# Down-projection of sixteen of 22 blocks by Strassen's scheme in two of three token groups

## The chip, the core and the metric

One core of a Trainium2 chip runs the whole program. The core has a matrix engine (TensorE, PE in the profile) that multiplies into PSUM banks, a vector engine (VectorE, DVE), a scalar engine (ScalarE, ACT), a helper (GpSimd, POOL), and a queue of transfers that is issued by SyncE (SP); a few transfers are issued by ACT. Each engine works off its own instructions in the order in which the program wrote them, and waits at semaphores for the others. The metric is the device time of one execution in microseconds; the median of the runs is given.

## The reference

One layer of a streaming encoder for 2048 prompt tokens and 64 sample tokens, width 1024, all in float32. First a mixer (pooling and mLSTM heads with an output projection), then a gated MLP with a causal depthwise convolution, then a final norm. Only the MLP matters here:

```python
h2 = rmsnorm(x, g2) * (1 + sc2) + sh2
up = h2 @ w_up
upp = jnp.concatenate([conv_buf.astype(up.dtype), up], 1)
conv = b_conv + sum(w_conv[j] * upp[:, j:j + T] for j in range(CONV_W))
a, g = jnp.split(conv, 2, -1)
x = x + gt2 * ((jax.nn.silu(g) * a) @ w_down)
```

`w_up` is 1024 x 5632 and `w_down` 2816 x 1024. The prompt and the sample have their own modulation (`gt2` and the rest), and the sample comes with its own convolution state.

## The kernel before

Rows of features lie on partitions, tokens along the free axis. Every product is made to float32 accuracy from two halves: a value is split into a rounded high part (by ACT) and what is left (by DVE), and three matmuls, high x high, high x low and low x high (`PASSES`), are summed in a PSUM bank. This holds for weights too: a unit of weights of 128 x 512 is loaded (`issue`), gets its high part on ACT at line 385 and its low part on DVE at line 388. `pump` keeps up to seven units loaded or on the way and works on the first four of them, so a weight unit is split some units ahead of its use.

The MLP takes the 2112 tokens in three groups of 704 (`fgroups`, `FT`), the last of which holds the 64 sample tokens at its end, so each row of its tokens has two segments (`o.segs`). The 2816 hidden features are 22 blocks of 128. A block needs an `a` and a `g` half, and these are made by a Strassen scheme of seven products (`Pair.products`, `product`, line 1544): 2 x 2 quarters of the input (token halves of 352 by feature halves) with the sums `B11, B21, T2, T3, B22, T1, T4` of `BN`, and the matching sums of the weights, which are kept in DRAM (`wsum`), two of the four already split (`wsplit`, `KEPT`). `copied`, `seed` and `plus` take the banks out on ACT and DVE, `conv_scale` and `conv_tap` make the convolution, `silu` and `gate` the gated block, `split_hi` and `split_lo` its two parts `av`. These steps of a block run behind the products of the next two blocks.

The down-projection is plain. The blocks of a group come in four parts of 5, 5, 6 and 6 (`PARTS`). After the products of a part come its 8 rows of outputs (`down`, line 1832): for each of the eight rows n, each block k and each token half the three matmuls, summed over the part's blocks in a bank, and `down_end` (line 1850) adds the bank times `gt2` to the row of x that lies in SBUF (`x3`). The steps of the part's last two blocks run during this stage, from a list `todo`; the last product `T4` of the last block is made after the first row.

Two background jobs are written into this order step by step, by `tick(0)` and `tick(1)`: `final` of the group before (its last norm and its store), and `prepare` of the next group (load x2, scale it, make the seven sums and their parts, store them to DRAM as `Bd` from line 813, with tiles of the pool `fscr`, six of them). `reload` brings them back. `tick(0)` comes twice in a product, `tick(1)` once in a block's products and in every second place of the down-projection.

PE, ACT, DVE and POOL keep the order in which the program was written (`manual_schedule`); the transfers on SP are placed by the scheduler. Six banks go round for products and down-projection; `begin_banks` writes all six once, so that a bank filled by ACT can be added to.

## Time and profile before

| | |
|---|---|
| median of 3 runs | 2208.43 us (2207.24 to 2209.56) |
| the profiled execution | 2208.32 us, span 2206.5 us, granted clock 0.998 |
| group 0 of the MLP | 797 to 1264.6 us of the span |
| group 1 | 1264.6 to 1729.8 us |
| group 2 | 1729.8 to 2206 us |

The profile is one execution. A row of the groups gives line, engine, operation, tile written and read, shapes, count, the busy time and the mean of one in nanoseconds, and the idle time before them with what ended it. Windows give the busy time of the engines in a stretch. Matmuls overlap in their pipeline, so the mean of one is longer than the step from one to the next.

### The profile page before, as it was taken

Reading aid. Unit: us, or ns where it says so; the run is one execution under the profiler, and the core shown is the slowest. Engines: PE = TensorE matmul, PEld = TensorE weight load, DVE = VectorE, ACT = ScalarE, POOL = GpSimd, SP = SyncE. Lnnn points to the kernel's source line nnn. Section 1 sums busy time; section 2 is a strip of 40 time slices with the busy share of each in tenths; the row PEclk is TensorE's granted clock in tenths of the full one; section 3 lists DMA queues with packets and bytes.
Section 4 is the critical chain, followed back from the end, with each engine's and each line's share of the span. In section 5 each row is a group of like instructions: output and inputs, shape, how many; then the busy total and the mean of one; then the engine's idle time right before and its main releaser. Section 6 shows DMA issues by size and latency. Waiting matters only on the chain.

```text
span 2206.5 us, 38048 instructions
## 1 busy us (share of the span) xinstructions
PE 2188.6 (99%) x13750; PEld 2085.7 (95%) x13750; DVE 1515.5 (69%) x2756; ACT 1053.3 (48%) x2113; POOL 213.1 (10%) x474
## 2 busy tenths in 40 slices
PE   8999999999999999999999999999999999999998
PEld 7888888888899999999999999999999999999998
DVE  5867668768855678686857577676656675757474
ACT  4554335334333456465636354645455453445264
POOL 0010000001000101010101210100001210101012
PEclk9999999999999999999999999999999999999999
DMA  8876998888878475657556875465448554353442
GB/s 322 328 292 229 310 301 276 303 287 269 300 254 289 148 273 165 242 170 273 180 196 212 282 263 183 154 216 200 151 156 290 193 177 167 115 173 113 152 145 81
DMA packets 274980, 487.06 MB, mean 221 GB/s; under 512 B 24640, under 2 KB 102976, under 8 KB 274792
## 3 DMA queue, kind: packets, MB, share of 16 engines
q1 hardware_dynamic: 265352, 462.32, 62.6%
q10 hardware_dynamic: 9440, 22.32, 2.6%
q8 instruction: 108, 1.77, 0.3%
q14 instruction: 80, 0.66, 0.1%
HBM read 378.48 MB, written 106.06 MB: 220 GB/s over the span
## 4 chain that ended last, share of the span: by engine, by line
PE 91%; DMA 4%; DVE 3%; issue 1%; ACT 1%; SPq 0%; POOL 0%; POOLq 0%; DVEq 0%; ACTq 0%
PE mm L1544 40%; PE mm L1832 23%; PE mm L451 20%; PE mm L1098 1%; DMA raw<-w_ada 1%; DMA wsum<-w 1%; PE m L1288 1%; PE m L1310 1%; PE m L1308 1%; DVE scr L243 1%; PE m L1273 1%; DVE wt L388 0%; DVE s L203 0%; PE mm L1035 0%; PE m L1263 0%
## 5 line engine op out<-in xcount | busy, mean ns | idle before, releaser
L1544 PE MATMUL mm<-hx,wt 128*128 128x352 f32 x5544 | 884.8, 321 | 1.4 <-DVE hx L751 1.4
L1544 PEld LDWEIGHTS mm<-hx,wt 128*128 128x128 f32 x5544 | 879.5, 188 | 2.3 <-DVE hx L751 1.7
L1832 PE MATMUL mm<-av,wt 128*128 128x352 f32 (+2 forms) x3168 | 511.8, 323 | 0.0
L1832 PEld LDWEIGHTS mm<-av,wt 128*128 128x128 f32 x3168 | 506.1, 188 | 2.0
L385 ACT ACTIVATE wt<-raw 128x512 fp32r<-128x512 f32 (+3 forms) x518 | 290.9, 573 | 253.8 <-PE mm L1832 128.6
L451 PE MATMUL mm<-hl,wt 128*128 128x512 f32 (+2 forms) x1920 | 386.1, 357 | 0.1
L388 DVE TENSOR_TENSOR wt<-raw,wt 128x512 fp32r<-128x512 f32 (+3 forms) x518 | 326.5, 640 | 81.0 <-ACT wt L385 80.8
L451 PEld LDWEIGHTS mm<-hl,wt 128*128 128x128 f32 x1920 | 315.4, 189 | 48.3 <-issue 5.3
L1850 DVE SCALAR_TENSOR_TENSOR x<-mm,MOD,x 128x352 f32<-128x352 f32 (+4 forms) x224 | 111.2, 526 | 136.4 <-PE mm L1832 136.4
L451 PE MATMUL mm<-mx,wt 128*128 128x512 f32 (+1 forms) x960 | 186.7, 356 | 0.0
L451 PEld LDWEIGHTS mm<-mx,wt 128*128 128x128 f32 x960 | 159.7, 188 | 26.1
L1531 DVE SCALAR_TENSOR_TENSOR tg<-eg,V,tg 128x704 f32<-128x704 f32 (+1 forms) x132 | 125.8, 953 | 69.4 <-ACT tg L1526 66.6
L1565 ACT ACTIVATE mm<-mm 128x352 f32<-128x352 f32 x132 | 59.1, 448 | 232.9 <-PE mm L1544 228.1
L1531 DVE SCALAR_TENSOR_TENSOR ta<-ea,V,ta 128x704 f32<-128x704 f32 (+1 forms) x132 | 125.7, 952 | 44.4 <-ACT ta L1526 24.6
L388 DVE TENSOR_TENSOR wt<-wt 128x512 fp32r<-128x512 f32 x176 | 117.0, 689 | 39.1 <-ACT wt L385 39.1
L385 ACT ACTIVATE wt<-wt 128x512 fp32r<-128x512 f32 x176 | 104.7, 622 | 11.8 <-DMA wt<-wsum 11.8
L1659 DVE TENSOR_TENSOR av<-tg,av 128x704 fp32r<-128x704 f32 (+1 forms) x88 | 60.5, 708 | 49.2 <-ACT av L1654 49.1
L1645 ACT ACTIVATE tg<-tg 128x704 f32<-128x704 f32 (+1 forms) x66 | 52.4, 794 | 69.9 <-DVE tg L1531 69.9
L1098 PE MATMUL mm<-wt,hl 128*128 128x256 f32 (+1 forms) x576 | 71.3, 284 | 0.0
L1098 PEld LDWEIGHTS mm<-wt,hl 128*128 128x128 f32 x576 | 70.4, 190 | 0.9 <-issue 0.6
L1649 DVE TENSOR_TENSOR tg<-ta,tg 128x704 f32<-128x704 f32 (+1 forms) x66 | 58.7, 890 | 16.1 <-ACT tg L1645 16.1
L1526 ACT ACTIVATE tg<-eg,V 128x704 f32<-128x704 f32 (+1 forms) x66 | 64.6, 978 | 3.3
(295 smaller groups left out, 1909.0 us busy)
## 6 DMA issues: line engine op xcount, KB each, us to landing
raw<-w_up SPq DMA_DIRECT2D x198, 256.0 KB, 3.4
wt<-hl_kept SPq DMA_DIRECT2D x96, 512.0 KB, 6.1
wt<-wsum SPq DMA_DIRECT2D x176, 256.0 KB, 4.2
wt<-wsplit SPq DMA_DIRECT2D x88, 512.0 KB, 4.2
raw<-w_down SPq DMA_DIRECT2D x96, 256.0 KB, 2.7
w<-w_up SPq DMA_DIRECT2D x88, 256.0 KB, 3.7
wsum<-w SPq DMA_DIRECT2D x44, 512.0 KB, 4.8
wsplit<-wt SPq DMA_DIRECT2D x44, 512.0 KB, 5.2
```

The source lines that it names most:

```text
L385: act.activation(u.w[:, 0, :u.n], u.raw[:, :u.n], AF.Copy)
L388: dve.tensor_tensor(out=u.w[:, 1, :u.n], in0=u.raw[:, :u.n], in1=u.w[:, 0, :u.n].bitcast(F32), op=ALU.subtract)
L451: pe.matmul(ps[bi][:, :hi - lo], U[:, a, k % 4 * P:(k % 4 + 1) * P], mv[k][:, b, lo:hi], start=(at == 0 and pi == 0), stop=(k == order[-1] ...
L1098: pe.matmul(ps[ti][:n, :cols], h[4 * kh + k4][:, b, lo:lo + n], U[:, a, k4 % 2 * cols:(k4 % 2 + 1) * cols], start=(kh == 0 and k4 == 0 and ...
L1526: act.activation(t[:, :E], ext[:, 2:2 + E], AF.Identity, scale=wc(2, f), bias=V[:, V_BC + f:V_BC + f + 1])
L1531: dve.scalar_tensor_tensor(out=t[:, :E], in0=ext[:, j:j + E], scalar=wc(j, f), in1=t[:, :E], op0=ALU.mult, op1=ALU.add)
L1544: pe.matmul(ps[:, :FH], U[:, a, kc * P:(kc + 1) * P], Bo.at(nm, kc, b), start=(first and kc == 0 and pi == 0), stop=(kc == 3 and pi == 2), ...
L1565: act.activation(to[:, :FH], ps[:, :FH], AF.Copy)
L1649: dve.tensor_tensor(out=self.tg[:, :E], in0=self.ta[:, :E], in1=self.tg[:, :E], op=ALU.mult)
L1659: dve.tensor_tensor(out=self.d[:, 1, a:b], in0=self.tg[:, a + 2 * s:b + 2 * s], in1=self.d[:, 0, a:b].bitcast(F32), op=ALU.subtract)
L1832: pe.matmul(ps[i][:, :hi - lo], U[:, a, k % 4 * P:(k % 4 + 1) * P], av[k][:, b, lo:hi], start=(k == 0 and (a, b) == PASSES[0]), stop=(k == ...
L1850: dve.scalar_tensor_tensor(out=x3[n][:, a:b], in0=ps[i][:, a - lo:b - lo], scalar=gt2(n, s), in1=x3[n][:, a:b], op0=ALU.mult, op1=ALU.add)
```

## The change

In groups 1 and 2 the parts become 4, 4, 4, 4 and 6 blocks; group 0 keeps its four. The last part of six is computed as before. A part of four blocks is two pairs of blocks, and its down-projection is done by Strassen's scheme: 2 x 2 quarters of the gated blocks (block of the pair by token half of 352) against 2 x 2 quarters of `w_down` (rows n and n + 4, block of the pair). Two runs (`duo`) of seven products with two half products each (rows 2d and 2d + 1), six matmuls in each half product. The results go from the banks into two or one places of x, by `rows_add` on DVE, and banks that serve two results are copied on ACT (`copy`).

The down-projection of a part (`quad_down`) stands behind the products of the next part's first block; that block's `T4` product is made inside it. The sums of the gated blocks are made by `step_2` to `step_6` in place of `split_hi` and `split_lo`. The weights come in a new order from the host (`w_quad`), and their sums are made in group 0 (`quad_sums`) and kept in DRAM (`dsum`).

Besides: a third of the kept sums of `w_up` is stored split; banks are taken and given back by name (`take`, `give`) where they went round; the one bank that needs it is opened alone; the plain parts are cut at 448 instead of 352 tokens; the pool `fscr` has four tiles instead of six, since `sums_of` works in place and in another order; `prepare` has two steps for each sum, and a block's products have three places of `tick(1)`; a half product of `quad_down` has one of each tick; `ta` and `tg` share three tiles; there are seven `av` tiles.

```diff
+AVB = 7
-HALVES = ((0, 352), (352, 704))
-PARTS = ((0, 5), (5, 10), (10, 16), (16, 22))
+PARTS = (((0, 5), (5, 10), (10, 16), (16, 22)),) + (((0, 4), (4, 8), (8, 12), (12, 16), (16, 22)),) * 2
...
-    KEPT = (WS2, WS1)
+    KEPT = (WS2, WS1, WS4)
...
+    def quad_units(p, first):
+        out = []
+        for d in (2 * p, 2 * p + 1):
+            raw, sums = [[(t[d, :, i], 512, place, None) for i in range(4)] for t, place in ((w_quad, OUT), (dsum, INSIDE))]
+            out += [raw[0], sums[WS1]] + first + [raw[1], sums[WS2], sums[WS3], sums[WS4], raw[3]]
+            first = []
+        return out
...
-        return spare[0].tile([P, FT], dt, tag="fscr", name="fscr", bufs=6)
+        return spare[0].tile([P, FT], dt, tag="fscr", name="fscr", bufs=4)
...
+        after = dict(B11=[(b11, b12, b11)], B22=[(b12, b22, b12), (b22, b22, b11)], T1=[(b21, b21, b22)])
+        place = dict(B11=b11, B21=b21, B22=b22, T1=b11, T3=b12, T2=b22, T4=b21)
+        for nm in ("B11", "B21", "B22", "T1", "T3", "T2", "T4"):
+            done()
+            hi, lo, end = put(nm)
+            act.activation(hi, place[nm], AF.Copy)
+            if slow:
+                yield
+            else:
+                low()
+            late.append((nm, place[nm], hi, lo, end))
+            if slow:
+                low()
+            yield
...
+    def quad_sums():
+        for d in range(8):
+            for c in (0, 256):
+                t = f2.tile([P, 2, FT], F32R, tag="av", name="qs", bufs=AVB)
...
+                nc.sync.dma_start(out=w, in_=w_quad[d, :, :, c:c + 256])
+                for _ in range(6):
+                    yield
+                a11, a12, a21, a22 = (w[:, i] for i in range(4))
+                dve.tensor_tensor(out=a22, in0=a21, in1=a22, op=ALU.add)
...
+                nc.sync.dma_start(out=dsum[d, :, :, c:c + 256], in_=w)
...
             product(b1, Bo, "B22", False)
-            rest((old, Pair.silu))
+            rest((old, Pair.silu), (older, Pair.step_6))
+            tick(1)
             product(b3, Bo, "T3", False)
...
+    def rows_add(o, n, lo, hi, bk):
+        for (a, b, s) in o.segs:
+            a, b = max(a, lo), min(b, hi)
+            if a < b:
+                dve.scalar_tensor_tensor(out=x3[n][:, a:b], in0=bk.t[:, a - lo:b - lo], scalar=gt2(n, s),
+                                         in1=x3[n][:, a:b], op0=ALU.mult, op1=ALU.add)
+
+    def quad_down(o, quad, cur, done):
+        done.gate()
+        done.step_2()
...
+            def half_product(nm, role, X, op, first=False):
+                if X == 0:
+                    pump()
+                    settle()
+                    units[nm] = get_unit()
...
+                for m in range(2):
+                    for pi, (a, b) in enumerate(PASSES):
+                        c = (2 * X + m) * P
+                        pe.matmul(bk.t[:, :FH], U[:, a, c:c + P], quad.put(op, m, b),
+                                  start=(first and m == 0 and pi == 0), stop=(m == 1 and pi == 2),
+                                  skip_group_check=not first)
+                    tick(m)
...
+            half_product("P1", "1A", 0, "B11", True)
+            if d == 0:
+                cur.sum_g1()
+                cur.sum_a()
+            half_product("P1", "1B", 1, "B11", True)
+            copy("2A", "1A")
+            if d == 0:
+                done.step_3()
+            half_product("P5", "3A", 0, "T1", True)
+            if d == 0:
+                done.step_4()
+            half_product("P5", "3B", 1, "T1", True)
+            add("3A", 0, (0, 1), (1, 1))
+            if d == 0:
+                cur.last_product()
+            else:
+                pump()
+            add("3B", 1, (0, 1), (1, 1))
+            half_product("P2", "2A", 0, "B21")
...
+            half_product("P6", "1A", 0, "T2")
+            copy("3A", "1A")
+            over("2A", 0, (0, 0))
...
+            half_product("P2", "2B", 1, "B21")
+            half_product("P6", "1B", 1, "T2")
+            copy("3B", "1B")
+            over("2B", 1, (0, 0))
+            half_product("P7", "3A", 0, "T3")
+            half_product("P3", "1A", 0, "B22")
+            add("3A", 0, (1, 1))
+            half_product("P7", "3B", 1, "T3")
+            over("1A", 0, (0, 1))
+            half_product("P3", "1B", 1, "B22")
+            add("3B", 1, (1, 1))
+            half_product("P4", "3A", 0, "T4")
+            over("1B", 1, (0, 1))
+            half_product("P4", "3B", 1, "T4")
+            over("3A", 0, (1, 0))
+            later.append(lambda: over("3B", 1, (1, 0)))
...
             for f in range(f0, f1_):
-                old, pair = pair, Pair(o, Bo, f, f - f0, av)
+                old, pair = pair, Pair(o, Bo, f, f - f0, av, quad)
                 pair.products(old)
...
+                if held is not None:
+                    quad_down(o, held, pair, old)
+                    held = None
```

`add` adds a bank to its places of x, and `over` does so and gives the bank back.

More of the change, by code (lines that the diff above doesn't have):

```diff
@@ L1536, in spans, with behind, product @@
         return [(pa, pb, a + 2 + 2 * s) for (i, pa, pb, a, b, s) in o.pieces if i == half]
-    def product(ps, Bo, nm, first):
+    later = []
+    def behind():
+        while later:
+            later.pop(0)()
+    def product(bk, Bo, nm, first):
         pump()
@@ L1558, in begin_banks, with __init__, start, take @@
[L1558 to L1565 removed]
+            act.activation(ext[:, d:d + b - a], bk.t[:, a:b], AF.Copy)
+    class Bank:
+        wide = 0
+        def __init__(self):
+            self.t = mm_ps()
+        def start(self, w):
+            self.wide = w
+    free = []
+    def take(seeded=False):
+        while len(free) + len(used) < 6:
+            free.append(Bank())
+        i = next((i for i, bk in enumerate(free) if bk.wide >= FH), 0) if seeded else 0
+        bk = free.pop(i)
+        used.append(bk)
+        if seeded and bk.wide < FH:
+            pe.matmul(bk.t[:, :FH], ones_r, B[-1].at("B11", 0, 0), start=True, stop=True)
+            bk.start(FH)
+        return bk
```

317 lines of the change are left out of this document (227 added, 90 removed).

## The prediction

> **What bounds the kernel now.** I read the busy times first, then who waited for whom on TensorE (PE) over the ConvFFN, then the chain of work that ended last, and last the windows of the stages that change.
>
> ```profile
> PE 2188.6 (99%) x13750; PEld 2085.7 (95%) x13750; DVE 1515.5 (69%) x2756; ACT 1053.3 (48%) x2113; POOL 213.1 (10%) x474
> ...
> PE mm L1544 <- DVE hx L751: 1.4, 1, 1.4
> PE m L1741 <- POOL rs L1683: 1.0, 1, 1.0
> PE m L1725 <- DVE m L1722: 0.9, 1, 0.9
> ...
> 1442.23 35.53 PE mm L1832 x222
> 1477.76 77.90 PE mm L1544 x492
> 1555.66 3.87 PE mm L1832 x24
> 1559.53 2.00 PE mm L1544 x12
> ```
>
> The three waits are all that PE has from 800 us to the end, 3.3 us in sum, none of them inside groups 1 and 2 before the last rows. The chain runs on PE alone there: products (L1544) and down-projection (L1832) take turns without a gap. So a matmul that goes takes its full interval with it, and whatever newly makes PE wait is paid in full. The intervals: 35.53 / 222 = 0.160 us at L1832, 77.90 / 492 = 0.158 us at L1544.
>
> ```profile
> 1012.40:1090.30 77.90, 77.90 (x494) 77.90 (x493) 57.27 (x84) 51.15 (x93) 7.92 (x20) 1.00 0.66 226
> 1264.60:1729.80 465.20, 465.20 (x2927) 464.87 (x2925) 314.51 (x490) 235.24 (x430) 43.92 (x97) 1.00 0.59 200
> 1331.70:1372.70 41.00, 41.00 (x258) 41.00 (x257) 31.24 (x59) 17.13 (x36) 0.68 (x4) 1.00 0.57 184
> 1372.70:1437.30 64.60, 64.60 (x410) 64.60 (x409) 42.51 (x62) 38.72 (x71) 7.39 (x16) 1.00 0.50 169
> 1729.80:2200.00 470.20, 468.30 (x2955) 465.91 (x2955) 296.17 (x537) 225.39 (x423) 69.14 (x192) 1.00 0.44 144
> ```
>
> Here each row is a stage: length, then busy PE, PEld, DVE, ACT, POOL, granted clock, DMA share, GB/s. Second and fifth are groups 1 and 2, third a down-projection, fourth a run of products, first a run of products of group 0. DVE has 68% in group 1 and 63% in group 2, 76% in the down-projection; ACT about half.
>
> **What PE loses.** A part of four blocks in groups 1 and 2 needs 4 x 8 x 3 x 2 = 192 matmuls of 352 columns by the old way; by the new one two runs of 14 half products of 6, so 168. Eight such parts: 192 fewer. 192 x 0.160 = 30.7 us. Of the six matmuls that opened the banks one is left: 5 x 0.16 = 0.8. The other blocks change from halves of 352 to 448 and 256 columns, which costs nothing:
>
> ```profile
> 2019.57 4.03 PE L1832 MATMUL mm<-av,wt 128*128 128x352 f32 x24
> ...
> 2145.59 4.03 PE L1832 MATMUL mm<-av,wt 128*128 128x448 f32 x24
> ```
>
> Both are 24 matmuls of equal columns in sum, the second half 448 and half 256. So PE's gain is 31.5 us, the floor 2208.3 - 31.5 = 2176.8. I sum against the profiled execution, 2208.32 us with a span of 2206.5; the median of the runs is 2208.43.
>
> **What DVE and ACT gain in work.** The rows:
>
> ```profile
> L388 DVE TENSOR_TENSOR wt<-raw,wt 128x512 fp32r<-128x512 f32 x195 | 136.9, 708 | 43.8 <-ACT wt L385 43.8
> L388 DVE TENSOR_TENSOR wt<-raw,wt 128x256 fp32r<-128x256 f32 x32 | 13.3, 416 | 0.0
> L388 DVE TENSOR_TENSOR wt<-raw,wt 128x128 fp32r<-128x128 f32 x32 | 9.0, 283 | 0.0
> L1850 DVE SCALAR_TENSOR_TENSOR x<-mm,MOD,x 128x352 f32<-128x352 f32 x89 | 50.2, 580 | 62.3 <-PE mm L1832 62.3
> L1850 DVE SCALAR_TENSOR_TENSOR x<-mm,MOD,x 128x288 f32<-128x288 f32 x24 | 12.3, 514 | 29.4 <-PE mm L1832 29.4
> L1850 DVE SCALAR_TENSOR_TENSOR x<-mm,MOD,x 128x64 f32<-128x64 f32 x32 | 8.8, 275 | 0.0
> L1659 DVE TENSOR_TENSOR av<-tg,av 128x704 fp32r<-128x704 f32 x22 | 19.6, 891 | 18.4 <-ACT av L1654 18.4
> L754 DVE TENSOR_TENSOR fscr<-fscr 128x352 f32<-128x352 f32 x4 | 2.1, 520 | 0.0
> ...
> L848 DVE TENSOR_TENSOR w<-w 128x256 f32<-128x256 f32 x44 | 18.5, 420 | 0.7
> ```
>
> For each of groups 1 and 2: adds into x 96 of 352 plus 16 for the last part against 64, about +28 us; halves and differences of the gated blocks (7 of 352 and 2 of 704 per pair of blocks, against 2 of 704) 56 x 0.52 = +29; weight units of 512: +32 x 0.71 less 16 x 0.28 and 8 x 0.42, +15; the third kept sum saves 22 x 0.71 = -16. Together +56, so DVE goes from 314 to 370 of 450 us, 82%, still under PE. ACT, about half busy, gains less than that. Group 0 gains 64 differences of the weights, 64 x 0.42 = 27 us, behind the ticks of its products, and 22 more stores of 512 KB. These edits I cost at nothing on the path because PE's own work covers them; if that cover is gone, it is the rivals' price below.
>
> **Where the cover is thin.** A DVE instruction's row is longer than the step to the next one:
>
> ```profile
> 1359.07 0.52 DVE L757 TENSOR_TENSOR fscr<-fscr 128x352 f32<-128x352 f32 x1
> 1359.50 0.52 DVE L751 TENSOR_TENSOR fscr<-fscr 128x352 fp32r<-128x352 f32 x1
> 1359.94 0.69 DVE L388 TENSOR_TENSOR wt<-raw,wt 128x512 fp32r<-128x512 f32 x1
> 1360.54 0.52 DVE L760 TENSOR_TENSOR fscr<-fscr 128x352 f32<-128x352 f32 x1
> ```
>
> Start to start a 352 takes 0.44, a 512 takes 0.60: 0.08 less than its row. So an add takes 0.50, a 704 takes 0.81. A stretch (quad_down: two runs, in the first the late product T4 of the next part's first block) takes PE 28 x 0.96 + 1.9 = 28.8 us. In the first run the tightest point is the last half product, P4 on bank 3B: it accumulates on a bank that DVE must have added to x after P7, and starts 1.9 + 13 x 0.96 = 14.4 us into the stretch. Queued on DVE up to that add: gate 0.81, four of 352 (1.76), two sums (0.88), two wide lows (1.62), seven weight lows (4.2), nine adds (4.5): 13.8 us. Margin 0.6 us if DVE enters with no debt, which the 42.5 of 64.6 us in the products' row allows. In the second run 10 us stand against 13.4, with room. In group 2 the cut at 2048 tokens splits the second half: each such add costs 0.43 + 0.20 - 0.50 = 0.13 more, seven of them, and 0.2 for gate and sums: 14.9 us, 0.5 late in each of four stretches, 2 us.
>
> Group 1 has worse: the preparation of group 2's input (prepare) now steps once per half product, where it had a step per two microseconds in the down-projection. In the first stretch its scaling of two rows (four instructions, 2.0 us) and six of 352 (2.6) fall ahead of the tight add: 4.6 - 0.6 = 4.0 us late; 4.2 more in the second run, 1 us over. In the second stretch 3.3 fall ahead: 2.7 late. The third and fourth have none. Two waits on transfers come with it:
>
> ```profile
> 1360.05 0.33 ACTq L813 DMA_DIRECT2D Bd<-fscr  x1
> 1361.52 0.33 ACTq L813 DMA_DIRECT2D Bd<-fscr  x1
> 1363.61 0.50 ACT L744 ACTIVATE fscr<-fscr 128x352 fp32r<-128x352 f32 x1 [2.02 <-DMA Bd<-fscr]
> ...
> Bd<-fscr ACTq DMA_DIRECT2D x56, 352.0 KB, 4.2
> fscr<-x2d SPq DMA_DIRECT2D x16, 352.0 KB, 5.9
> ```
>
> A scratch tile is free 3.5 us after its store was issued (1360.05 to 1363.61), and ACT stands still meanwhile: behind it queue the copies from bank to bank and the high halves of the weights, and PE waits for both. Before, PE did not notice. With four scratch tiles instead of six and steps a microsecond apart the same waits come while copies are due within 1 to 2 us. The next rows of x2d land 5.9 us after issue and are asked for two steps, 2 us, later: up to 4 us with DVE standing in its queue. No row prices this on PE; its bounds are 0 and 4 us in each of two stretches. I take 3 and 2, since the trace's two nearest waits are both over 2.
> Hand-overs between engines are not in the sums: 0.5 us a stretch, 4 us.
> Sum of waits: 4.0 + 1 + 3 + 2.7 + 2 + 2 + 4 = 18.7 us. Forecast 2176.8 + 18.7 = 2195.5, given as 2195.
>
> ```profile
> 2186.00:2206.00 20.00, 13.56 (x104) 12.79 (x102) 9.18 (x26) 4.89 (x12) 6.44 (x9) 0.81 0.39 144
> ```
>
> In the last 20 us, where PE has gaps, the granted clock is 0.81; in the groups it is 1.00. A stretch that stalls could bring the same: 0.19 x 20 = 3.8 us lost after it. [...]
>
> **The rivals.**
> 1. No wait shows: DVE's debt is paid from slack everywhere. For it: PE has not waited once in 936 us, and DVE has 18% left. Against: the margin of 0.6 us. 2177 to 2182. Chance 0.22.
> 2. The forecast, waits of 6 to 27 us: 0.48.
> 3. DVE's queue becomes the bound in every stretch, and the kernel is slower. It decides from 31.5 / 8 = 3.9 us per stretch. For it: with full rows instead of steps, 25 instructions x 0.08 = 2.0 us more stand in the first run, so 1.4 late in each of group 1's two quiet stretches, 2.5 in each of group 2's four, and with both transfer waits at their 4 us 11.0 and 8.7 where prepare runs: 32.5, and 4 for hand-overs, 2213. With the clock at 0.81 for 20 us behind each stretch, 8 x 3.8 = 30 us come on top of the forecast: 2226. Against: the steps are measured. Chance 0.18, of which the clock 0.05.
> 4. The gain is made and given back in group 0: 22 more stores and 32 transfers of 512 KB on SP's queue, 27 us of DVE in stages already at 57 of 78 us and DMA 0.66. Ten to fifteen us lost there: 2206 to 2211. Against: the slack of 20 us per stage. Chance 0.12.
>
> **How the numbers follow.** What can be told from no change is 0.2%, 4.4 us: faster is under 2204, slower over 2213. Faster takes cases 1 and 2: 0.70. Case 4 and a rest of 3 are within: 0.13. Slower 0.17. The range: below, rival 1 with some hand-overs left out, 2179; above, rival 3 with full rows, 2213. The forecast's own range is 2183 to 2204.
>
> **What would show it.** PE should have 192 fewer matmuls at L1832's successors and no gap in group 0; its waits should lie in the stretches, most in the first two of group 1, named by DVE adds into x (or ACT copies) and there by x2d and Bd; group 2's stretches about 1 us each. DVE should stand near 82% in group 1. Wrong it is if waits appear in the products, if group 2's stretches wait over 3 us, or if the clock falls below 1.00 there.

## The result, and the profile after

| | median (range, runs) | profiled execution |
|---|---|---|
| before | 2208.61 us (2205.97 to 2210.98, 20) | 2208.32 us |
| changed | 2212.51 us (2206.56 to 2218.33, 20) | 2218.33 us, span 2216.5 us |

The ratio is 1.0016, 95% interval 1.0009 to 1.0023: 3.9 us longer, which the interval sets apart from no change but which lies inside the 0.2% that the prediction counts as none. It had forecast 2195 us. The profiled execution of the changed kernel is the longest of its twenty, 5.8 us above the median; so its stages are read here, and whether they hold is left to the runs behind them.

First the busy times of the changed kernel and the windows of its three groups (the third runs on into the kernel's tail, as before's did). The columns are those of the prediction's windows. Line 1567 is now the block's product, 2003 the half product of `quad_down`, 2123 the plain down-projection, 1614 the copy from bank to bank, 1977 the add into x, 409 and 412 a weight's high and low half.

```profile
PE 2174.7 (98%) x13553; PEld 2052.6 (93%) x13553; DVE 1634.7 (74%) x3040; ACT 1093.6 (49%) x2181; POOL 239.5 (11%) x474
```

```profile
801.84:1274.75 472.91, 468.90 (x2922) 459.41 (x2921) 359.24 (x594) 259.32 (x469) 48.26 (x95) 1.00 0.81 275
1274.75:1750.17 475.42, 460.82 (x2831) 453.00 (x2830) 361.10 (x580) 255.51 (x473) 52.16 (x97) 0.99 0.64 221
```

PE has 13553 matmuls against 13750: 192 + 5 fewer, as counted. But group 1, whose 465.2 us should have lost 15.7 (half of 31.5), is 475.4 long, group 0 is 472.9 against 465.9 of before, and only group 2 is shorter: 459.6 against 469.7 (from its first product at 1750.17 to the start of the last matmuls at 2209.78). Who waited, in the list of PE's waits (total, times, longest):

```profile
PE mm L2003 <- ACT mm L1614: 11.3, 11, 3.0
...
PE mm L1567 <- ACT mm L1614: 2.8, 3, 2.2
PE mm L1567 <- DVE hx L764: 2.6, 3, 1.3
...
PE mm L2003 <- DVE x L1977: 1.8, 3, 1.0
PE mm L1567 <- DVE wt L412: 1.5, 2, 1.0
...
PE mm L2003 <- DVE ea L1576: 0.9, 2, 0.5
```

The name that leads is ACT's copy from bank to bank, not DVE's add into x. The four stretches of group 1 in the windows, and the stage of products behind the second:

```profile
1341.40:1378.60 37.20, 32.23 (x187) 30.91 (x186) 32.61 (x62) 19.27 (x40) 1.32 (x2) 0.95 0.63 210
1432.80:1468.80 36.00, 31.06 (x182) 28.58 (x181) 32.49 (x62) 17.94 (x37) 1.31 (x2) 1.00 0.73 243
1526.50:1557.00 30.50, 29.43 (x182) 28.76 (x181) 26.32 (x48) 13.79 (x28) 1.32 (x2) 1.00 0.62 209
1608.00:1638.00 30.00, 29.76 (x186) 29.28 (x185) 25.59 (x46) 13.38 (x27) 1.32 (x2) 1.00 0.54 185
1468.80:1526.50 57.70, 54.50 (x326) 53.92 (x325) 43.14 (x69) 35.14 (x65) 5.55 (x14) 0.97 0.57 201
```

Against the 28.8 us that PE needs, the first two lose 8.4 and 7.2, the other two 1.7 and 1.2 (the last 0.7 by PE's own rows, which run from 1608.33 to 1637.81). In the first two DVE holds 62 instructions and 32.5 us of rows, more than PE's 28.8; prepare is what they have and the others have not. ACT is about half busy in all of them, and still it is ACT that PE waits for. The timeline of ACT, and under it that of DVE and of PE, at the longest wait (start, length, what it did, and in brackets the idle time before it and its releaser):

```profile
1351.31 1.07 ACT L730 ACTIVATE fscr<-fscr,MOD 128x640 f32<-128x640 f32 x2 [4.00 <-DVE fscr L728]
1352.29 0.44 ACT L1580 ACTIVATE eg<-mm 128x352 f32<-128x352 f32 x1
1352.76 0.45 ACT L1614 ACTIVATE mm<-mm 128x352 f32<-128x352 f32 x1
```

```profile
1348.82 1.07 DVE L1977 SCALAR_TENSOR_TENSOR x<-mm,MOD,x 128x352 f32<-128x352 f32 x2
1349.80 0.68 DVE L412 TENSOR_TENSOR wt<-wt 128x512 fp32r<-128x512 f32 x1
1350.40 1.07 DVE L728 SCALAR_TENSOR_TENSOR fscr<-fscr,G,rb 128x640 f32<-128x640 f32 x2
```

```profile
1353.26 8.54 PE L2003 MATMUL mm<-av,wt 128*128 128x352 f32 x42 [3.04 <-ACT mm L1614]
```

That is the chain in small. Prepare scales a row on DVE (L728) and adds its shift on ACT (L730), both written in one step. DVE has no idle time and comes to the scaling late, behind four adds. ACT stands 4.00 us at the shift, and behind it in ACT's queue stand two instructions whose inputs had long been ready, the second the copy that PE needs. So ACT's order hands on DVE's delay to a bank that doesn't depend on it.

The second long wait, in the second stretch, has the other cause that the prediction named:

```profile
1460.81 8.23 PE L2003 MATMUL mm<-av,wt 128*128 128x352 f32 x48 [2.24 <-ACT mm L1614]
```

In ACT's timeline the copy stands at 1460.31, behind two steps of prepare, the first of which (1458.45) had stood still for 3.02 us for a store of `Bd` out of a scratch tile. So an engine and a store can both hold ACT's queue.

A wait has a second price, in windows of 3.4 us around two of them:

```profile
1350.60:1354.00 3.40, 0.74 (x4) 0.74 (x5) 3.40 (x8) 2.65 (x6) 0.00 (x0) 1.00 0.00 0
1354.00:1357.40 3.40, 3.40 (x14) 3.40 (x13) 1.92 (x5) 2.69 (x7) 0.00 (x0) 0.51 0.22 77
1357.40:1360.80 3.40, 3.40 (x22) 3.40 (x22) 2.74 (x7) 1.64 (x5) 0.00 (x0) 0.99 0.86 257
...
1480.30:1483.70 3.40, 3.40 (x14) 3.40 (x13) 3.33 (x6) 2.38 (x5) 0.49 (x1) 0.50 0.00 0
```

After waits of 3.04 and 2.23 us (the second is in the products, at 1479.26) the granted clock is half for 3.4 us, and 14 matmuls go in that time in place of 22: 8 x 0.16 = 1.3 us more for each. After the wait of 2.24 us shown above it stays at 1.00; the last section comes back to this.

### The profile page after: what moved, and what is told of

It reads as the page before. It is cut to its first block, busy times and chain, and to the rows that moved or that the text cites. A ratio compares the mean times of both kernels' runs of the same rounds, so it can differ in the third digit from the quotient of the medians.

```text
span 2216.5 us, 38099 instructions
## 1 busy us (share of the span) xinstructions
PE 2174.7 (98%) x13553; PEld 2052.6 (93%) x13553; DVE 1634.7 (74%) x3040; ACT 1093.6 (49%) x2181; POOL 239.5 (11%) x474
## 4 chain that ended last, share of the span: by engine, by line
PE 82%; DVE 7%; DMA 6%; issue 2%; ACT 2%; SPq 1%; POOL 0%; DVEq 0%; ACTq 0%; POOLq 0%
PE mm L1567 36%; PE mm L475 21%; PE mm L2123 12%; PE mm L2003 6%; DVE wt L412 2%; DMA raw<-w_ada 2%; PE mm L1112 1%; DVE x L1977 1%; DMA Bd<-fscr 1%; PE m L1302 1%; PE m L1322 1%; PE m L1324 1%; DMA wsum<-w 1%; DMA hl_kept<-wt 1%; PE m L1287 1%
## 5 line engine op out<-in xcount | busy, mean ns | idle before, releaser
L409 ACT ACTIVATE wt<-raw 128x512 fp32r<-128x512 f32 (+3 forms) x470 | 276.7, 597 | 182.7 <-PE mm L475 72.1
L412 DVE TENSOR_TENSOR wt<-raw,wt 128x512 fp32r<-128x512 f32 (+3 forms) x470 | 312.7, 671 | 58.1 <-ACT wt L409 57.9
L2123 PE MATMUL mm<-av,wt 128*128 128x448 f32 (+1 forms) x1632 | 262.6, 322 | 0.0
L2123 PEld LDWEIGHTS mm<-av,wt 128*128 128x128 f32 x1632 | 250.4, 188 | 11.1
L2003 PE MATMUL mm<-av,wt 128*128 128x352 f32 x1344 | 226.2, 326 | 14.5 <-ACT mm L1614 11.3
L2003 PEld LDWEIGHTS mm<-av,wt 128*128 128x128 f32 x1344 | 216.6, 189 | 21.8 <-ACT mm L1614 14.5
L1977 DVE SCALAR_TENSOR_TENSOR x<-mm,MOD,x 128x352 f32<-128x352 f32 (+3 forms) x360 | 168.5, 505 | 78.6 <-PE mm L2123 60.9
L1614 ACT ACTIVATE mm<-mm 128x352 f32<-128x352 f32 x196 | 87.2, 447 | 247.4 <-PE mm L1567 204.7
L412 DVE TENSOR_TENSOR wt<-wt 128x512 fp32r<-128x512 f32 x196 | 132.9, 684 | 18.9 <-ACT wt L409 18.8
L409 ACT ACTIVATE wt<-wt 128x512 fp32r<-128x512 f32 x196 | 119.2, 622 | 32.1 <-DMA wt<-wsum 30.1
L1523 POOL COPY ea<-UC 128x2 f32<-128x2 f32 x66 | 34.6, 524 | 516.2 <-DVE ta L1545 506.7
```

Of the source, the lines that this page charges most:

```text
L409: act.activation(u.w[:, 0, :u.n], u.raw[:, :u.n], AF.Copy)
L412: dve.tensor_tensor(out=u.w[:, 1, :u.n], in0=u.raw[:, :u.n], in1=u.w[:, 0, :u.n].bitcast(F32), op=ALU.subtract)
L1523: pool.tensor_copy(ext[:, 0:2], UC[:, f, :])
L1614: act.activation(to.t[:, :FH], bk.t[:, :FH], AF.Copy)
L1977: dve.scalar_tensor_tensor(out=x3[n][:, a:b], in0=bk.t[:, a - lo:b - lo], scalar=gt2(n, s), in1=x3[n][:, a:b], op0=ALU.mult, op1=ALU.add)
L2003: pe.matmul(bk.t[:, :FH], U[:, a, c:c + P], quad.put(op, m, b), start=(first and m == 0 and pi == 0), stop=(m == 1 and pi == 2), skip_grou ...
```

## The experiments

Group lengths are read from the start of a group's first product in PE's timeline to the next group's, the last one to the start of the last matmuls. Each is from one execution, often one of the longer ones of its kernel, so a difference of a microsecond or two between two kernels means little by itself. "Ideal" is before less half of 31.5 us for each of groups 1 and 2. Every kernel ran beside runs of before (their medians lie between 2208.61 and 2210.30 us), against which its ratio is taken. The letters of the theories are those of each expectation.

| kernel | median (range, runs) | ratio to before, 95% interval | group 0 | group 1 | group 2 |
|---|---|---|---|---|---|
| before | 2208.61 | 1 | 465.9 | 465.2 | 469.7 |
| ideal | | | 465.9 | 449.5 | 454.0 |
| changed | 2212.51 | 1.0016 (1.0009 to 1.0023) | 472.9 | 475.4 | 459.6 |
| last group only | 2201.76 (2201.42 to 2205.78, 6) | 0.9970 (0.9959 to 0.9981) | 469.5 | 465.4 | 459.6 |
| two kept sums | 2217.71 (2211.08 to 2220.80, 6) | 1.0034 (1.0022 to 1.0047) | 471.9 | 477.3 | 460.2 |
| prepare in the products | 2202.75 (2198.74 to 2206.91, 8) | 0.9968 (0.9958 to 0.9978) | 471.9 | 465.0 | 459.6 |
| shift later | 2205.94 (2201.88 to 2210.82, 11) | 0.9987 (0.9979 to 0.9996) | 472.0 | 469.1 | 460.2 |
| half pace | 2202.46 (2199.23 to 2207.06, 10) | 0.9968 (0.9959 to 0.9978) | 469.3 | 466.2 | 459.6 |
| half pace, shift later | 2198.74 (2196.65 to 2203.31, 5) | 0.9955 (0.9942 to 0.9967) | 469.5 | 463.4 | 461.3 |
| no weight sums in group 0 | 2209.12 (2205.88 to 2213.60, 11) | 1.0000 (0.9991 to 1.0009) | 465.9 | 474.7 | 459.6 |
| T4 later | 2206.50 (2203.12 to 2208.65, 11) | 0.9984 (0.9975 to 0.9992) | 473.1 | 472.9 | 455.6 |
| three edits | 2195.55 (2192.69 to 2198.08, 5) | 0.9930 (0.9918 to 0.9942) | 471.3 | 462.5 | 455.6 |
| three edits, sums on POOL | 2209.46 (2204.26 to 2212.82, 12) | 0.9994 (0.9986 to 1.0003) | 480.3 | 462.5 | 455.7 |
| steps in the second run, sums begin later | 2195.14 (2191.04 to 2198.50, 5) | 0.9928 (0.9914 to 0.9941) | 471.9 | 464.3 | 455.6 |
| three edits, no differences | 2193.82 (2190.91 to 2197.34, 5) | 0.9928 (0.9916 to 0.9941) | 467.8 | 462.5 | 455.8 |
| in the products, with the orders mended | 2197.62 (2195.10 to 2198.81, 5) | 0.9941 (0.9928 to 0.9955) | 469.2 | 461.4 | 455.6 |

**Which group pays.** Group 1's parts are left plain, as they were before; only group 2 has the scheme:

```diff
-PARTS = (((0, 5), (5, 10), (10, 16), (16, 22)),) + (((0, 4), (4, 8), (8, 12), (12, 16), (16, 22)),) * 2
+PARTS = (((0, 5), (5, 10), (10, 16), (16, 22)),) * 2 + (((0, 4), (4, 8), (8, 12), (12, 16), (16, 22)),)
-    return g > 0 and part[1] - part[0] == NQ
+    return g > 1 and part[1] - part[0] == NQ
```

> Strassen's down-projection in group 2 alone; group 1 has its four plain parts again. Theory A (group 1 gives back all it gains, by 10 us more than all): group 1 takes 465 us as before the change, group 2 457-458 as in the changed kernel, median 2202-2206. Theory B (what is lost is lost in group 0 and by DVE's sum of work): group 2 stays near 458 but group 1 is above 470, median 2210 or more.

Group 2 keeps its 10 us, group 1 is back at 465.4, the median is 2201.76. So the scheme does make time where prepare doesn't run beside it, and its second use gives all of that back. Group 0, whose code is that of the changed kernel, stays 3.6 us above before.

**The third kept sum.** One of the changed kernel's additions, the third of the weight sums that is stored already split, is taken out:

```diff
-    KEPT = (WS2, WS1, WS4)
+    KEPT = (WS2, WS1)
```

> Only the third kept sum of the up weights is undone: 22 stores of 512 KB less in group 0, and 22 splits more in groups 1 and 2 each. Theory A (group 0 lost its 5 us to the stores together with the weight sums, DMA share 0.94): group 0 goes from 473 us back to 468-470, groups 1 and 2 grow by 0 to 3 us each because DVE has 15 us more: median 2209-2213. Theory C (group 0's loss is the weight sums alone): group 0 stays at 472 or more and the median rises by 1-4 us.

Group 0 isn't restored by 22 fewer stores of 512 KB (471.9), and the median is 5.2 us higher. The extra stores are not what group 0 pays for; the split that they save seems to help.

**Prepare out of the stretches.** Prepare makes no step inside group 1's stretches, and two more in each block's products:

```diff
             product(b1, Bo, "T2", False)
+            if o.g == 1:
+                tick(1)
             seed(b3, b1)
...
             product(b3, Bo, "T3", False)
+            if o.g == 1:
+                tick(1)
...
-                    tick(m)
+                    if m == 0 or o.g != 1:
+                        tick(m)
```

> The preparation of group 2's input no longer steps inside group 1's Strassen stretches; two more steps stand in each block's products of group 1 instead. Theory A (these steps cost group 1 its gain: DVE and ACT in the first two stretches, and the products after them): group 1 of the span goes from 475 us to 455-458, the first two stretches from 37.2 and 36.0 us to about 30 each like the third and fourth, and the median from 2212.5 to 2193-2198. Theory B (the loss is that DVE has more work in sum, wherever it stands): the waits move into the products, group 1 stays above 468 and the median above 2207.

Group 1 gets 10.4 us shorter, and not the 17 to 20 of theory A; 465.0 lies between the two theories. The waits moved along with prepare, into the products, and one step now stood ahead of a `seed`, the products' own copy from bank to bank, the same place in ACT's queue as in the stretches. So neither the stretch itself nor DVE's sum of work is enough to explain it, and the next runs take the two apart.

**The shift behind the scaling.** DVE keeps its order. Only ACT's shift comes a tick or two later:

```diff
             for x, k in zip(xs, (kc, kc + 4)):
-                normed(x, k, o.t0, FT, box[0])
+                normed(x, k, o.t0, FT, box[0], "scale")
                 yield
+            yield
+            for x, k in zip(xs, (kc, kc + 4)):
+                normed(x, k, o.t0, FT, box[0], "shift")
```

> The only edit: the two steps in which prepare scales a row on DVE stay where they are, and the two ACT instructions that add the shift (which in the changed kernel stand right behind them in ACT's queue and waited 4.0 us for DVE there) come one and two ticks later, with one more tick for each pair of rows. DVE's queue keeps its order and its work. Theory A (ACT stands still for DVE, and the copies from bank to bank and the high halves of the weights queue behind it): the waits of PE for ACT's bank copies in the first two stretches of group 1 (3.0, 0.9, 2.2, 2.2 us) fall to under 1 us each, group 1 goes from 475.4 to 464 to 468 us, median 2200 to 2206. Theory B (DVE has 32.5 us of work in a stretch for which PE needs 28.8, so PE waits for DVE whatever ACT does): the waits stay or change their name to DVE, group 1 473 to 476, median 2210 to 2214.

Group 1 is 469.1, between the two theories' numbers: 6.3 us came from ACT's order alone, the wait of 3.04 us is gone, and 20 us over the ideal remain. What the longest wait is now, in the timelines of ACT and PE:

```profile
1364.61 0.50 ACT L780 ACTIVATE fscr<-fscr 128x352 fp32r<-128x352 f32 x1 [2.05 <-DMA Bd<-fscr]
1365.01 0.45 ACT L1619 ACTIVATE mm<-mm 128x352 f32<-128x352 f32 x1
```

```profile
1365.51 4.17 PE L2008 MATMUL mm<-av,wt 128*128 128x352 f32 x24 [2.07 <-ACT mm L1619]
```

Again a copy (here L1619) behind an instruction of prepare, which this time waits for a scratch tile that a store still reads.

**Half the pace.** Prepare takes a step in every second half product of group 1's stretches, so its work reaches over all four and the products between:

```diff
-                    tick(m)
+                    if m == 0 or X == 1 or o.g != 1:
+                        tick(m)
```

> In group 1's stretches prepare takes a tick only in the second half product of each product, 14 in place of 28 a stretch, so its work is spread over all four stretches and the products between them. Theory B: DVE's load in a stretch falls from 32.5 to about 29 us, no stretch is over 30.5 us, group 1 goes from 475.4 to 455 to 459 us, median 2192 to 2197. Theory A: every pair of rows still makes ACT stand behind DVE once, now in four stretches in place of two, so the first two lose about half of their 7 to 8 us and the last two lose more than their 1.5 us of now: group 1 464 to 470, median 2201 to 2207.

466.2 us and 2202.46: A's lower half, 7 us above what B gives. Spreading the work is worth 9 us, but doesn't reach B's stretches. Both edits at once:

> Both edits together: half the ticks for prepare in group 1's stretches, and the shift on ACT one and two ticks behind the scaling on DVE. Theories A and B both expect the best group 1: 453 to 458 us, against 449.5 without any wait, median 2190 to 2197. If it is not below the better of the two single edits by 2 us, the two causes are one and the same wait. If group 1 stays over 462, neither is the cause, and the transfers (stores of Bd out of four scratch tiles) are left.

463.4 us, 2.8 below the better one alone, and the medians are 3.7 apart; so each has its own share. Together they don't reach 453 to 458. By the expectation's last clause, over 462, neither would be the cause; that goes too far, since 12.0 of group 1's 25.9 us over the ideal are gone, but something else is left as well.

**The same order in group 2.** There prepare doesn't run, and every stretch has one wait of 0.73 us ahead of P7. In ACT's timeline of the changed kernel, and under it in PE's:

```profile
1826.27 0.50 ACT L1765 ACTIVATE av<-tg 128x352 fp32r<-128x352 f32 x1 [2.12 <-DVE tg L1772]
1826.67 0.61 ACT L409 ACTIVATE wt<-raw 128x512 fp32r<-128x512 f32 x1
1827.19 0.79 ACT L1614 ACTIVATE mm<-mm 128x352 f32<-128x352 f32 x2
```

```profile
1827.69 19.47 PE L2003 MATMUL mm<-av,wt 128*128 128x352 f32 x120 [0.73 <-ACT mm L1614]
```

The high half of T4, needed last of all in the stretch, waits for a difference on DVE, and the copy to bank 3A stands behind it. The run moves that one instruction:

```diff
             self.less(b21, b21, b11)
-            self.hi("T4", b21)
+
+        def step_5b(self):
+            if self.quad is not None and self.second:
+                self.hi("T4", self.blocks()[2])
...
             copy("3A", "1A")
+            if d == 0:
+                done.step_5b()
```

> The changed kernel with one ACT instruction moved: in a stretch's first run the high half of T4 (step_5), which waits 2.1 us for DVE, stands ahead of the copy from bank 1A to 3A in ACT's queue; here it stands behind that copy, DVE's queue is unchanged. Theory A (ACT's order): in group 2, where prepare does not run, the wait of 0.73 us ahead of P7 goes from all four stretches, group 2 goes from 459.6 to 456.5 to 457.2 us; group 1 gains 1 to 4 us, median 2205 to 2209. Theory B (DVE late): the wait stays or moves to the next half product, group 2 stays at 459 to 460, median 2211 to 2214.

455.6 us, a little better than theory A's range: all four waits are gone, and group 2 is 1.6 us above its ideal. The median, 2206.50, is in A's range too. This is the cleanest of the runs: no work was taken away and DVE's queue is the same. With the two edits on prepare:

> Half the ticks for prepare in group 1's stretches, its shift behind its scaling, and the high half of T4 behind the copy to 3A. Theory A expects every wait for a bank copy in the stretches to fall below 0.4 us: group 2 456.5 to 457.2, group 1 from 463.4 to 458 to 461, median 2192 to 2196. What is then left of the ideal 449.5 and 454 is DVE's (its adds into x and the weights' low halves in the first run), which theory B would see unchanged: group 2 459 to 461, group 1 462 to 464, median 2197 to 2200.

2195.55 us, 17 us under the changed kernel and 14.7 under before beside it (2210.30): three changes of order and pace, with no work taken away, beat both kernels. Group 1 is 462.5, at B's end. Its waits, from the list:

```profile
PE mm L2011 <- DVE wt L412: 2.4, 3, 1.2
PE mm L2011 <- DVE x L1985: 2.3, 3, 1.0
...
PE mm L2011 <- ACT mm L1619: 1.4, 3, 0.5
```

ACT's copies cost 1.4 us where they had cost 11.3. What is left in the stretches is named by DVE.

**Where prepare's steps should stand.** Two runs ask what is left in group 1. In the first, the stretch's 14 steps all come in its second run, where the prediction had found room on DVE (the other edit of this kernel is read below):

```diff
-                    if m == 0 or X == 1 or o.g != 1:
+                    if m == 0 or d == 1 or o.g != 1:
                         tick(m)
...
-        if o.g == 0:
-            bg[0].append(quad_sums())
...
                 pair.products(old)
+                if o.g == 0 and f == 1:
+                    bg[0].append(quad_sums())
```

> The kernel with three edits (half pace, shift later, T4 later), with two things placed otherwise: the 14 ticks of a stretch for prepare in group 1 all come in its second run, where the prediction found 10 us of DVE against 13.4, and none in its first run; and the sums of the down-projection's weights in group 0 begin two blocks later. Theory B for what is left in group 1 (DVE's queue in the first run): the waits there for weights' low halves, for ea and for x go, group 1 goes from 462.5 to 457 to 460 us. If it stays at 462 to 463, the pace in the first run isn't what is left. Group 0: if its loss sits at its start (2.4 us of waits for the input's low halves), it goes from 471.3 to 468 to 469.5; if it sits in what the sums themselves do, it stays at 469.5 to 472. Median 2190 to 2193 with both, 2195 to 2197 with none.

464.3 us, above what either case expects: the stretches' waits for weights are gone, and in their place ACT stands still for a store, in ACT's timeline:

```profile
1526.83 0.50 ACT L780 ACTIVATE fscr<-fscr 128x352 fp32r<-128x352 f32 x1 [3.97 <-DMA Bd<-fscr]
1527.23 0.61 ACT L409 ACTIVATE wt<-wt 128x512 fp32r<-128x512 f32 x1
1527.75 0.44 ACT L1619 ACTIVATE mm<-mm 128x352 f32<-128x352 f32 x1
```

Denser steps meet the four scratch tiles, and PE waits 2.12 us at 1528.25. In the second run the steps stand in the products, all of them behind the copies, with the orders of the three edits:

> Prepare makes no step in group 1's stretches; its steps stand in the products, five a block, each behind the copies from bank to bank, its shift behind its scaling, and the high half of T4 behind the copy to 3A. What is open: group 1 of the kernel with three edits still has 462.5 us, 7 us more of waits than group 2, which has no prepare. Theory B for the rest (prepare's work on DVE inside the stretches, whatever ACT's order): without it the stretches are those of group 2, about 0.5 us lost each; in the products DVE has the room, group 1 goes to 453 to 457 us, median 2187 to 2192. Theory A for the rest (an ACT instruction of prepare that waits, for DVE or for a store of Bd, stands ahead of a copy wherever it is put): the waits move into the products as they did when the steps were put there without the other two edits (group 1 465.0), group 1 459 to 464, median 2193 to 2198.

461.4 us, theory A's range; the median can't be told from that of the three edits. The stretches are nearly clean, and the products wait instead:

```profile
1423.26 1.23 PE L2015 MATMUL mm<-av,wt 128*128 128x352 f32 x6 [0.34 <-DVE ea L1581]
1488.96 13.93 PE L1572 MATMUL mm<-hx,wt 128*128 128x352 f32 x82 [1.20 <-DVE wt L412]
...
1655.64 28.13 PE L1572 MATMUL mm<-hx,wt 128*128 128x352 f32 x166 [1.89 <-DVE wt L412]
```

At the last of these DVE had itself stood still, 4.13 us, for the convolution's first step on ACT (line 1545), which came behind prepare's four shifts, 2.02 us of rows. So it runs both ways: ACT's queue holds DVE, and DVE is then late with the weights. Wherever prepare is put, group 1 keeps 12 to 15 us over its ideal. More scratch tiles, or no prepare at all, weren't tried, so how these are shared between the stores and the two queues stays open.

**Group 0.** In three runs its length answers. First, the weight sums are left out; groups 1 and 2 read other sums of the same size, so their work is the same:

```diff
-        if o.g == 0:
-            bg[0].append(quad_sums())
...
-            raw, sums = [[(t[d, :, i], 512, place, None) for i in range(4)] for t, place in ((w_quad, OUT), (dsum, INSIDE))]
+            raw, sums = [[(t[d, :, i], 512, place, None) for i in range(4)] for t, place in ((w_quad, OUT), (wsum, INSIDE))]
```

> Leaves out the sums of the down-projection's weights in group 0 (64 differences on DVE, 16 loads and 16 stores of 256 KB a half); groups 1 and 2 read the sums of the up-projection's weights from DRAM instead, units of the same size, so the values are wrong and the work of groups 1 and 2 is the same. Theory C (these sums and their transfers cost group 0 its 6 us, the fourth rival of the prediction): group 0 goes from 472 to 466 to 467 us, median 2206 to 2208. Theory D (group 0 loses by the new order of its own input's sums at its start, and by products that step at 0.1667 in place of 0.1583 us whatever the weights' sums do): group 0 stays at 469 to 473, median 2210 to 2213.

465.9, the length of before, 7 us under the changed kernel; the medians are 3.4 apart, and 2209.12 lies between the two theories. Not all of the 7 can be the sums'. The changed kernel's first difference runs at 826.6 us of its span. By the matmuls of the row sums, which end the group's start (818.52 us there), 2.3 us over before are already lost, and this start is 14.7 to 16.7 us long in the kernels with the sums, 14.3 in before and 13.7 here. Behind it the group takes 456.2 us in the changed kernel, 451.6 in before and 452.1 here, so 4.1 us go with the sums in this execution. Of these, 2.6 lie in one stage of products, which takes 80.5 us in place of 77.9 without a recorded wait (last section); "last group only" and "half pace" make the same sums and take 77.9 there. Then the sums stay, but the 64 differences are left out (the three edits are in both):

> The kernel with three edits, without the 64 differences of the down-projection's weights (27 us of DVE in group 0); the loads of 512 KB and the stores stay, and what is stored are the weights themselves, so the output is wrong and groups 1 and 2 do the same work. If DVE's work is what costs group 0 its 4 to 6 us, it goes from 471.3 to 466 to 467.5 us, as without any sums, and the median from 2195.6 to 2191 to 2193. If the 32 transfers of 512 KB cost it, group 0 stays at 469.5 to 472 and the median at 2194 to 2197.

467.8 against 471.3, just above the first range; behind the start 452.8 against 455.3. Group 0 measures 469.2 to 473.1 in the eleven profiles that have these sums on DVE, so its own scatter is 4 us; 467.8 is below them all. Behind the start, 2.5 us go with the differences and 0.7 is left over the kernel without sums. DVE's differences are the larger part in this pair, then, and how much the transfers have is not settled: the slower stage is in both (80.2 us), and neither before nor the kernel without the sums has it there. The medians, 1.7 us apart over five runs each, can't tell it. Last, the differences are made by POOL:

```diff
-                dve.tensor_tensor(out=a22, in0=a21, in1=a22, op=ALU.add)
+                pool.tensor_tensor(out=a22, in0=a21, in1=a22, op=ALU.add)
```

(and the same for the other three).

> The kernel with the three edits above, and the 64 differences of the down-projection's weights in group 0 made by POOL in place of DVE; their loads and stores stay. If DVE's 27 us are what costs group 0 its 4 to 6 us (2.5 us of it waits in its first 10 us, for the low halves of its input), group 0 goes from 469 to 472 to 466 to 467 us and the median is 2.5 to 5 us under the kernel without this edit. If the transfers are what costs it (products that step at 0.1667 us under a DMA share of 0.93), group 0 stays at 469 to 473 and the median is the same within 1.5 us.

A miss on both sides: group 0 is 9 us longer, 480.3. Why, in the timelines of POOL, DVE and PE:

```profile
980.47 1.07 POOL L1635 TENSOR_TENSOR qs<-qs 128x256 f32<-128x256 f32 x1
981.61 0.91 POOL L1637 TENSOR_TENSOR qs<-qs 128x256 f32<-128x256 f32 x1
982.46 0.48 POOL L1528 COPY eg<-UC 128x2 f32<-128x2 f32 x1
```

```profile
979.71 1.23 DVE L412 TENSOR_TENSOR wt<-raw,wt 128x512 fp32r<-128x512 f32 x1
980.86 1.05 DVE L766 TENSOR_TENSOR fscr<-fscr 128x352 fp32r<-128x352 f32 x1
```

```profile
985.29 1.98 PE L1572 MATMUL mm<-hx,wt 128*128 128x352 f32 x11 [1.55 <-DVE eg L1581]
```

While POOL subtracts, these DVE instructions take nearly twice their time (1.23 and 1.05 against 0.69 and 0.52 in the prediction's rows); the three weight lows that start at 982.83, behind POOL's last difference, take 1.88 us together. Over group 0 DVE is busy for 358.2 us with 530 instructions, against 359.2 with 595 in the three edits, where the differences are on DVE itself: of the 27 us, 1 was taken off.
The run that began the sums two blocks later left group 0 at 471.9, with 2.1 us of waits for its input's low halves as ever: its start is not where the sums cost. What makes the start longer or shorter is open.

## Why the prediction was wrong

**The floor held.** 197 matmuls went, and where the waits were taken away the time came: group 2 with T4 later is 14.1 us under before, of 15.7.

**The loss over the floor was forecast as 18.7 us and is 41.8 in the profiled execution** (35.7 at the median, 2212.5 - 2176.8): 25.9 in group 1 (475.4 - 449.5), 5.6 in group 2 (459.6 - 454.0), 7.0 in group 0, and 3.3 ahead of the MLP (first product at 801.8 us against 798.5). The last can't be put to the change: the same start falls between 798.1 and 801.8 in the other kernels. Term by term:

| | forecast | measured |
|---|---|---|
| group 1, stretch 1 (4.0 + 1 + 3 + 0.5) | 8.5 | 8.4 |
| group 1, stretch 2 (2.7 + 2 + 0.5) | 5.2 | 7.2 |
| group 1, stretches 3 and 4 | 1.0 | 2.9 |
| group 1, products | 0 | 7.4 |
| group 2 | 4.0 | 5.6 |
| group 0 | 0 | 7.0 |

The stretches were forecast at 18.7 and cost 24.1, in the order named (the first two of group 1 worst) and with the releasers named (DVE, ACT copies, Bd). That the first comes to 8.4 against 8.5 is in part luck: PE waited 3.9 us there for ACT's copies and 1.0 for DVE's add, where 5.0 of the forecast were DVE's; the clock's 1.3 and four matmuls of prepare (0.65) make up some of the rest. The step that failed is "These edits I cost at nothing on the path because PE's own work covers them". It was said of group 0, and by silence of group 1's products; the two lost 14.4 us, and the fourth rival, at 0.12 chance, was the right one for a part of the first. With the 5.4 us by which the stretches went over, that is 19.8 us, more than the 12.8 us of gain that the forecast left. Two of the prediction's own signs of being wrong came, waits in the products and a clock below 1.00 (0.95 in the first stretch).

**Group 0.** The rival's mechanism happened, at less than half its price: behind the start 4.1 us over the kernel without the sums in this execution, 1.4 to 5.0 over the kernels with these sums on DVE, and not 10 to 15. "The slack of 20 us per stage" was the wrong measure: a stage with DVE at 57 of 78 us has room on average, and still in the three edits PE waited 0.87 and 0.93 us (at 966 and 980 us) for DVE's step on the `g` half (`eg`), and without the differences neither wait is there. The 2.3 us of the start aren't explained.

**Group 1's products.** Behind the second stretch the stage took 57.7 us, where its 27 products need 324 x 0.158 = 51.3; behind the first 54.2 (1378.60 to 1432.80). That is 6.4 and 2.9, 9.3 in sum. The table's 7.4 is only what the stretches leave over, and these are counted too long there: four matmuls of prepare in the first (0.65 us) are work, and the fourth's window is half a microsecond too wide. The one long wait there, 2.23 us, again for a copy on ACT, is prepare's end reaching past the stretch, with the clock's 1.3 behind it; the forecast let prepare's cost end with the stretch. Most of the rest comes without a recorded wait (last section).

**Hand-overs, 0.5 us a stretch.** In group 2 a stretch lost 1.4, where the forecast had 0.5 for hand-overs, which was the author's estimate and stands in no row, and 0.5 for DVE's adds. One instruction's place in ACT's queue was 0.73 of it with some follow-on: moving it gave 4.0 us over four stretches. The forecast counted ACT as half busy and let its queue stand still for stores alone, not for DVE; here it was as late as the latest thing that it waited for.

**Margin at P4 on 3B.** The tight point was named as the last half product; PE's long waits came at P2 on 2B and P7 on 3A, both seeded by ACT. At P4 PE did wait for DVE's add into x, 1.01 us in the first stretch and 1.8 in three waits in all, under the 6.7 forecast for the first runs of the two stretches. With the orders mended it is 2.3 us in three, so the DVE count was a limit, but not the first.

**The clock.** The forecast's sum has nothing for it; a lower clock stood in the third rival alone. Two single waits, of 3.04 and 2.23 us, were each followed by 3.4 us at half, 1.3 us each, so some 2.6 us of the forecast's error. The third rival in turn came out near the measured median, 2213, but not by its mechanism: it has DVE late in every stretch, and group 2's, which it puts at 2.5 us late each, lost 1.4, most of it to ACT's order. That the number fits is luck.

## What to carry to other kernels

Ask of each instruction of a background job not only what its engine has to do, but what it will wait for and what is written behind it: an engine that is half idle delays the critical path when a waiting instruction stands ahead of a ready one (ACT, busy for 49% of the span, held PE for 11.3 us in the changed kernel's stretches), and here it cost nothing to write it a step later (group 2 got 4.0 us shorter). Let no edit be free because an engine has room on average: give it the price of the nearest critical instruction in the same queue. And a saving of PE's work has to be tested stage by stage, since here one group kept it and the next gave it back.

## What the runs showed of the hardware

The granted clock fell to 0.50 to 0.56 for one window of 3.4 us after waits of 3.04, 2.23 and 1.87 us. After one of 2.07 us, and after the one of 2.24 us in the changed kernel, it stayed at 1.00, so a single wait's length doesn't decide it. The rows of the waits of 2.07 and 1.87 us, of the kernel with the shift later:

```profile
1365.50:1369.00 3.50, 3.49 (x21) 3.41 (x22) 3.50 (x8) 2.42 (x5) 0.00 (x0) 1.00 0.68 266
1453.70:1457.10 3.40, 3.38 (x12) 3.14 (x12) 2.06 (x5) 1.36 (x3) 0.00 (x0) 0.56 0.59 235
```

With T4 later PE's rows show the same:

```profile
1360.92 15.15 PE L2006 MATMUL mm<-av,wt 128*128 128x352 f32 x90 [2.23 <-DVE x L1980]
...
1455.67 9.49 PE L2006 MATMUL mm<-av,wt 128*128 128x352 f32 x48 [1.72 <-ACT mm L1614]
```

Behind the wait of 1.72 us 48 matmuls took 9.49 us, where 48 took 8.23 behind the 2.24 us of the changed kernel; behind the wait of 2.23 us 90 took 15.15, where 90 took 14.87 in the three edits. What decides it was not shown.

A product's step has two values at full clock and without a recorded wait. Two windows of the changed kernel, and under them PE's row of the same stage in the kernel "last group only":

```profile
1020.90:1040.90 20.00, 20.00 (x129) 20.00 (x128) 12.43 (x23) 10.58 (x21) 1.17 (x3) 1.00 0.95 323
1050.00:1100.00 50.00, 50.00 (x302) 50.00 (x301) 44.42 (x71) 35.19 (x63) 6.57 (x16) 1.00 0.98 353
```

```profile
1016.84 78.07 PE L1567 MATMUL mm<-hx,wt 128*128 128x352 f32 x492
```

50.00 / 302 is 0.166 us, 20.00 / 129 is 0.155, and 78.07 / 492 is 0.159, which before's rows of 492 show too. Heavy transfers alone don't decide it: the DMA share is 0.95 in the first window, which has the faster step, and 0.56 from 1402 to 1432 us of the changed kernel, where 182 matmuls take 30.00 us, 0.165 each. In the starts of the changed kernel's single matmuls the slower step is 166 or 167 ns each time and the faster one goes round from 155 to 162. In two kernels the slower one sets in behind a wait: one of 0.49 us in "steps in the second run, sums begin later" (264 matmuls in 42.13 us before it, 228 in 38.23 behind it) and one of 0.93 us in "three edits, no differences" (384 in 61.17, then 108 in 18.26). In the changed kernel and in the three edits no recorded wait stands ahead of it (492 in 80.65 and 80.38 us). It stays to the end of the stage, 50 us in the changed kernel, which costs 2.6 us. What starts it and keeps it is open.
